# The second matrix of an MLP in seven half-block products, with weight sums formed in DRAM

## The chip, the core and the metric

The kernel runs on one core of a Trainium2 chip. Its time is the device time of one execution in microseconds; lower is better. A core has five engines which run side by side and wait for one another by semaphores: TensorE (PE in the profile) multiplies matrices, VectorE (DVE), ScalarE (ACT) and GpSimd (POOL) work element by element, SyncE (SP) issues transfers. Transfers (DMA) are issued on an engine's queue, in order with what that engine does, and are carried out by 16 DMA engines. Products land in PSUM, which has eight banks of 128 x 512 float32; all else lies in SBUF, and the inputs in DRAM.

## The reference

The input is a sequence of 1024 tokens with 1024 features, and there are two layers. Each layer is a mixer and an MLP, each followed by a layer norm of the scaled residual:

```
for layer in range(2):
    mix = hybrid_mixer(x, ...) if layer == 0 else recurrent_mixer(x, ...)
    x = layer_norm(ALPHA * x + mix, ln1_g[layer], ln1_b[layer])
    h = relu(x @ w1[layer])                    # 1024 -> 4096
    x = layer_norm(ALPHA * x + (h * h) @ w2[layer], ln2_g[layer], ln2_b[layer])   # 4096 -> 1024
```

The hybrid mixer joins windowed attention and a gated delta rule; the recurrent mixer is a gated branch beside a short convolution and a linear recurrence. All of it is float32. For each token half and layer the MLP is two products: 512 x 1024 by 1024 x 4096, and 512 x 4096 by 4096 x 1024.

## The kernel before, in words

**Two halves as two streams.** The 1024 tokens are cut into two halves of 512 (c = 0 and c = 1). `stream(c)` is a Python generator that emits, in order, a half's hybrid mixer, output projection and layer norm (`mix_out`), first MLP and norm (`mlp_ln`), four recurrent blocks (`rec_block`), their output projection and norm, and the second MLP and norm. The driver at the end of `trunk` takes turns between the two streams: a stream in phase 0 (a mixer) goes before one in phase 1 (first MLP) or 2 (second MLP), and of two in the same phase the first half goes first; in the recurrent blocks (`light`) the two change places after every unit. A generator that lacks a buffer or a condition yields `BLOCK`, and the other stream goes on; one that has finished a unit yields `UNIT`. So the MLP of one half lies between the products of the other half's mixer and fills the time in which those wait. Small pieces of work (layer norm, attention, the delta rule) are "mixers": generators that are asked first whenever a planner thinks their operands are there.

**The planner.** `Clock` keeps a rough model of the engines and gives every product a place in one fixed order on TensorE (`_pe`, a scheduling-only dependency on the product before). The other engines' orders come from the framework's scheduler; it is not bound to the order of emission.

**Products in float32 out of three.** TensorE runs a one-pass format (float32r). Every operand is split into a rounded part h and a rest l, and `mm3` (lines 359 to 362; the profile records the products at L204) issues h·h, h·l and l·h: three products of 128 x 128 by 128 x 512 for each block. `wblock` brings a weight stage of 128 x 1024 into one of three buffers `ws` on SyncE's queue, rounds it into `wh` (ScalarE, every fifth half on VectorE) and subtracts it into `wl` (VectorE and GpSimd in turn), in two halves of 512 columns; there are four half buffers of each. All instructions on the elementwise engines and all DMA issues are recorded at one line of the profile (L177), so they are told apart by tile names: `ws`, `wh`, `wl` weights; `g` the large buffers (activations, residuals); `s`, `t`, `f` rings of 128 x 512; `mm`, `mx` the two groups of four PSUM banks; `lns`, `lnw` norm statistics; `w` in a DMA stands for all MLP weights.

**The MLP** (`mlp`). It goes through eight parts e of 512 hidden units. For each, four projections by the first matrix, of eight `mm3` or 24 products each (`proj_fm`) give the hidden units; ScalarE takes relu and square, GpSimd squares again in float32, VectorE takes the rest l. Then for each of two column halves of the output, two weight stages with 16 `mm3`, 48 products, follow, summed in four banks; VectorE adds each bank to the residual `y`. In the last part of the very last MLP the order is turned, so that the final norm can start with the first 128 tokens.

**The norm** (`layernorm`). Statistics come with the last additions; then passes on VectorE, ScalarE and GpSimd; then 32 transposes on TensorE, after which ScalarE and VectorE split each bank into h and l for the next product.

**What the change touches**: `wblock`, `mm3`, `proj_fm`, `mlp`, `out_proj`, `rec_block`, `mix_out`, `mlp_ln`, `stream`, the planner's DMA entry, the rings' sizes, and the layout of w2 in DRAM.

Of the kernel before, what the change touches and what calls it, by code (L numbers as in the profile page):

```python
# [27 lines left out]
WB, HV, LG = 4, 5, 2  # L28
RINGS = dict(t=11, s=9, f=4)
# [29 lines left out]
class Clock:  # L59
    """Orders the tensor engine's work by a rough model of the engines: when each product's operands will be there."""  # L60
# [103 lines left out]
    def engine(self, eng, key):  # L164
        clk = self

        class Engine:
            def __getattr__(self, op):
                f = getattr(eng, op)

                def call(*a, **k):
# [6 lines left out]
                    if op == "dma_start":  # L178
                        clk.issue("D", outs, ins, max(0.06, aps[0].nbytes() / 360e3), 0.0, 2.0)
                        return r  # L180
# [20 lines left out]
    def matmul(self, out, lhsT, rhs, start, stop):  # L201
        n = int(np.prod(rhs.shape[1:]))
        c = 0.00042 * n * (1 if rhs.dtype == F32R else 4) if lhsT.shape[-1] > 32 else 0.046
        return self._pe(self.pe.matmul(out, lhsT, rhs, start=start, stop=stop), out, [lhsT, rhs], c, start)  # L204
# [6 lines left out]
def trunk(ctx: ExitStack, tc, I, out):  # L211
# [3 lines left out]
    DS, DA = clk.engine(nc.sync, "V"), clk.engine(nc.scalar, "V")  # L215
# [32 lines left out]
    def tl(r, dt=F32):  # L248
        return take(r, tpool.tile([P, 516], dt, tag=r, name=nm(r), bufs=RINGS[r]))

# [88 lines left out]
    def wblock(src, n=1024, hl=None):  # L339
        st = clk.tile("ws", 3, wpool.tile([P, 1024], F32, tag="ws", name=nm("ws"), bufs=3))[:, :n]  # L340
        DS.dma_start(st, src)
        m = n // 2
        if hl is None:
            hl = [clk.tile(t, WB, wpool.tile([P, 512], F32R, tag=t, name=nm(t), bufs=WB))[:, :m] for _ in range(2) for t in ("wh", "wl")]
        for i in range(2):
            h, l = hl[2 * i:2 * i + 2]
            a = st[:, i * m:(i + 1) * m]
            wcount[0] += 1
            if wcount[0] % HV == 0:
                V.tensor_copy(h, a)  # L350
            else:
                S.copy(h, a)
            if wcount[0] % LG == 0:
                G.tensor_tensor(l, a, h, ALU.subtract)
            else:
                V.tensor_tensor(l, a, h, ALU.subtract)
        return ([hl[0], hl[2]], [hl[1], hl[3]])

    def mm3(ps, lh, ll, rh, rl, start, stop):
        PE.matmul(ps, lh, rh, start=start, stop=False)  # L360
        PE.matmul(ps, lh, rl, start=False, stop=False)
        PE.matmul(ps, ll, rh, start=False, stop=stop)
# [34 lines left out]
    def load_xT(c, x, k2):  # L397
# [5 lines left out]
        else:  # L403
            st = clk.tile("ws", 3, wpool.tile([P, 1024], F32, tag="ws", name=nm("ws"), bufs=3))[:, :1024]
# [7 lines left out]
    def proj_fm(src, x, bank=None):  # L412
        wh, wl = wblock(src)
# [86 lines left out]
    def mlp(layer, yT, yg, ls, res=None):  # L500
        w1, w2 = I[f"w1_{layer}"], I[f"w2_{layer}"]
        for e in range(8):
            sh, sl = [], []
            yield from need("s", 9)
            wb, own = [], []
            if e == 7 and res is not None:
                yield from need("g", 4)
                for b in range(4):
                    t = gran(F32R)
                    own.append(t)  # L510
                    wb.append(wblock(w2[e * 4 + b], hl=[t[:, i * 512:(i + 1) * 512] for i in range(4)]))
            for f in range(4):
                ps = yield from proj_fm(w1[e * 4 + f], yT)
                h, l, r = ts("s", F32R), ts("s", F32R), ts("s")
# [4 lines left out]
                free("s", r)  # L519
                sh.append(h)  # L520
                sl.append(l)
                if e == 7 and f == 3:
                    yT.free()
                yield UNIT
            if e == 7 and res is not None:
                for n in range(NT):
                    a, b = n * P, (n + 1) * P
                    for half in range(2):
                        ps = mm_ps()
                        for f in range(4):  # L530
                            wh, wl = wb[half * 2 + f // 2]
                            mm3(ps, sh[f][:, a:b], sl[f][:, a:b], wh[f % 2], wl[f % 2], f == 0, f == 3)
                            yield
                        y = ytile(yg, n)[:, half * 512:(half + 1) * 512]
                        V.tensor_tensor(y, y, ps, ALU.add)
                        V.bn_stats(ls[:, n, 6 * half:6 * half + 6], y)
                    res["n"] = n + 1
                    if n == 0:
                        res["start"]()
                    yield UNIT  # L540
                free("g", *own)
                free("s", *sh, *sl)
                return
            for half in range(2):
                ps = [mm_ps() for _ in range(NT)]
# [790 lines left out]
```

## Time and profile before

| | |
|---|---|
| time, median of 3 runs | 2387.01 us (2386.92 to 2388.69) |
| span of the profiled execution, first to last instruction | 2384.5 us |
| mean granted TensorE clock | 0.992 |
| instructions | 33354 |
| moved by DMA | 227.43 MB, mean 95 GB/s |
| HBM read, written | 216.89 MB, 8.39 MB |

The profiled execution has no time of its own apart from its span; the 2.5 us between the span and the median lie around the first and the last instruction. The page gives each engine's busy time, its share of the span and its count of instructions. PEld is the loading of the stationary operand, which overlaps the products. In a row of a group the fields are: line, engine, operation, tile written <- tiles read, sizes, count | busy time in us, mean ns of one | idle time of the engine just before them <- what ended it. A row of the chain of waits has who waited, for whom, the total in us, how often, and the longest. In a row of a stretch, the count of instructions follows each engine's busy time. In a row of the timeline, start and length in us come first. In 40 equal slices of the span PE is at 90% or more in all but the first three, the seventh and the last.

```
PE   8889997999999999999999999999999999999997
DVE  7697659565754463755664623455665543633345
ACT  5364424443333242454443322344554232322331
POOL 3342334232332243433443432343333333433341
```

### The profile page before, as it was taken

The page shows a single profiled execution, that of the slowest core. Times are in us where ns is not written, and L with a number is a line of the kernel's source. Part 1 is how long each engine was busy: PE and PEld are TensorE (multiplying, and loading weights), DVE is VectorE, ACT ScalarE, POOL GpSimd, SP SyncE. Part 2 cuts the span into 40 slices and gives each one's busy share as a digit, 9 for nine tenths or more (in the row PEclk, how much of TensorE's full clock was granted, in tenths as well). Part 3 has the DMA queues.
Part 4 walks back from the last instruction along what each step waited for, and adds up shares of the span by engine and source line. Part 5 has one row for each costly group of instructions (what it writes and reads, how often), then busy time and mean ns, then how long its engine had stood idle before and what let it go on. Part 6 is the DMA issues. An engine that isn't in the chain of part 4 may idle for free. (4 is left out here: it accounts for less than half of the span.)

```text
span 2384.5 us, 33354 instructions
## 1 busy us (share of the span) xinstructions
PE 2298.9 (96%) x12724; PEld 1841.9 (77%) x12724; DVE 1345.1 (56%) x2550; ACT 912.7 (38%) x1813; POOL 843.0 (35%) x706
## 2 busy tenths in 40 slices
PE   8889997999999999999999999999999999999997
PEld 7666775677777878778887788877887788778876
DVE  7697659565754463755664623565665543633345
ACT  5364424443333242454443322344554232322331
POOL 3342334232332243433443432343333333433341
PEclk9999998999999999999999999999999999999999
DMA  4121231122233222322333222232325222332231
GB/s 154 54 81 31 81 124 36 54 69 74 73 114 110 95 88 98 123 89 97 98 131 125 82 96 97 97 121 91 98 93 177 85 97 97 107 115 98 98 117 51
DMA packets 67487, 227.43 MB, mean 95 GB/s; under 512 B 7424, under 2 KB 7808, under 8 KB 67328
## 3 DMA queue, kind: packets, MB, share of 16 engines
q1 hardware_dynamic: 58832, 204.01, 25.9%
q10 hardware_dynamic: 8496, 21.30, 2.5%
q8 instruction: 100, 1.64, 0.3%
q14 instruction: 59, 0.48, 0.1%
HBM read 216.89 MB, written 8.39 MB: 94 GB/s over the span
## 5 line engine op out<-in xcount | busy, mean ns | idle before, releaser
L177 POOL TENSOR_TENSOR wl<-ws,wh 128x512 fp32r<-128x512 f32 (+1 forms) x372 | 497.6, 1338 | 1261.4 <-ACT wh L177 979.4
L204 PE MATMUL mm<-g,wh 128*128 128x512 f32 x2816 | 886.7, 396 | 0.5 <-DVE g L177 0.5
L177 ACT CAST wh<-ws 128x512 fp32r<-128x512 f32 (+1 forms) x595 | 365.5, 616 | 993.0 <-PE mm L204 910.1
L204 PE MATMUL mm<-wh,s 128*128 128x512 f32 x1984 | 648.2, 399 | 11.4 <-ACT s L177 5.7
L204 PEld LDWEIGHTS mm<-g,wh 128*128 128x128 f32 x2816 | 520.2, 189 | 107.2 <-issue 2.9
L204 PE MATMUL mm<-g,wl 128*128 128x512 f32 x1408 | 550.9, 391 | 5.4 <-POOL wl L177 5.4
L204 PEld LDWEIGHTS mm<-wh,s 128*128 128x128 f32 x1984 | 374.0, 189 | 102.6 <-ACT s L177 6.2
L204 PE MATMUL mm<-wl,s 128*128 128x512 f32 x992 | 391.9, 395 | 2.3 <-POOL wl L177 1.4
L177 DVE TENSOR_TENSOR wl<-ws,wh 128x512 fp32r<-128x512 f32 (+1 forms) x372 | 281.2, 756 | 188.8 <-ACT wh L177 184.4
L204 PEld LDWEIGHTS mm<-g,wl 128*128 128x128 f32 x1408 | 265.1, 188 | 64.0 <-POOL wl L177 7.1
L204 PE MATMUL mm<-wh,g 128*128 128x512 f32 (+1 forms) x768 | 235.2, 380 | 10.0 <-ACT wh L177 6.1
L177 DVE TENSOR_TENSOR s<-s,s 128x512 fp32r<-128x512 f32 x128 | 100.4, 784 | 242.9 <-POOL s L177 231.1
L204 PEld LDWEIGHTS mm<-wl,s 128*128 128x128 f32 x992 | 187.4, 189 | 43.3 <-POOL wl L177 1.8
L177 DVE TENSOR_TENSOR g<-g,mm 128x512 f32<-128x512 f32 x224 | 144.0, 680 | 130.7 <-PE mm L204 130.5
L204 PEld LDWEIGHTS mm<-wh,g 128*128 128x128 f32 x768 | 142.0, 190 | 38.7 <-ACT wh L177 6.1
L177 DVE CAST wh<-ws 128x512 fp32r<-128x512 f32 (+1 forms) x149 | 73.8, 495 | 172.6 <-PE mm L204 165.0
L177 POOL TENSOR_TENSOR s<-s 128x512 f32<-128x512 f32 x128 | 145.3, 1135 | 26.4 <-ACT s L177 26.4
L204 PE MATMUL mm<-wl,g 128*128 128x512 f32 (+1 forms) x384 | 143.7, 374 | 0.1
L177 ACT ACTIVATE s<-mm 128x512 f32<-128x512 f32 x128 | 75.9, 593 | 62.1 <-PE mm L204 61.9
L177 ACT ACTIVATE s<-s 128x512 fp32r<-128x512 f32 (+1 forms) x136 | 83.5, 614 | 19.0 <-DVE s L177 8.0
L204 PEld LDWEIGHTS mm<-wl,g 128*128 128x128 f32 x384 | 72.9, 190 | 11.9 <-DVE wl L177 0.4
L204 PE MATMUL mx<-g,wh 128*128 128x512 f32 x256 | 78.8, 389 | 0.0
(209 smaller groups left out, 2230.3 us busy)
## 6 DMA issues: line engine op xcount, KB each, us to landing
ws<-w SPq DMA_DIRECT2D x256, 512.0 KB, 3.3
ws<-hin_fm SPq DMA_DIRECT2D x32, 512.0 KB, 3.3
ws<-rin SPq DMA_DIRECT2D x32, 512.0 KB, 3.3
ws<-hout SPq DMA_DIRECT2D x16, 512.0 KB, 3.4
ws<-rout SPq DMA_DIRECT2D x16, 512.0 KB, 3.4
t<-ln ACTq DMA_DIRECT2D x28, 256.0 KB, 4.2
ws<-hin_q SPq DMA_DIRECT2D x8, 512.0 KB, 3.2
g<-x ACTq DMA_DIRECT2D x8, 512.0 KB, 5.0
```

Of the source, the lines that this page charges most:

```text
L177: r = f(*a, **k)
L204: return self._pe(self.pe.matmul(out, lhsT, rhs, start=start, stop=stop), out, [lhsT, rhs], c, start)
```

## The change

**The second matrix in seven products.** A block j is two parts e: 1024 hidden units. Its product, 512 tokens by 1024 units by 1024 columns, is cut in two along each of the three: A (units by tokens) into a11, a12, a21, a22 and the weights into b11, b12, b21, b22. Instead of eight quarter products there are seven (`seven`), each of 256 tokens by 512 units by 512 columns, 24 products of TensorE: two weight stages, two chunks of 128 units each, two token tiles, three products. The activation sides are combined on VectorE in place (four combinations of 128 x 1024); the weight sides are four sums and differences t1 to t4 which are formed beforehand. Partial results stay in PSUM (two banks X of the `mm` group, two banks R of `mx`), later products add to them, and VectorE adds or subtracts a bank to the residual after each product.

**Hidden units kept raw.** For such a block `hidden` keeps the squared hidden units in float32 in two large buffers, and the split into h and l is made for each product of the seven (ScalarE copy and VectorE subtract of 128 x 512, twice per product). GpSimd has no part in it: the weight subtracts of `hidden` and `seven` are all on VectorE.

**Woven.** `weave` emits one unit of the next block's first matrix (24 products) and then two units of the present block's seven (12 products each). The last block of an MLP has no next one; in the last MLP of the second half `ends` and `finish` take the place of the turned order of before, and part 6 goes first in the old way.

**Which blocks.** An MLP goes part by part in the old way (`straight`) until e is even, two large buffers are free, and, for the first half, the second half's output projection of the same layer has been emitted; the rest goes in blocks of seven products.

**Sums in DRAM.** `w2_sums` is started as a mixer with the first MLP. For each layer and block it copies a quarter of w2 (1 MiB) into each of t1 to t4 on SyncE's queue, then adds further quarters by accumulating DMAs on GpSimd's queue (four, then two, then one), with the planner's clock between them.

**Order of the stages.** The recurrent blocks of the second half no longer wait until the first half's are done, but for the same block of the first half; they use ring `s`. The second half's norm before an MLP (`hold`), and the first half's norm after its first MLP, wait until the other half has emitted the last product of its first matrix.

**Weight stages.** `wblock` casts and subtracts 1024 columns at once, with three buffers of 1024 instead of four of 512. Ring `s` has 10 tiles instead of 9; a pair of tiles `r` is new; the descriptor scratch for GpSimd's DMAs is set to 2048 bytes.

```diff
-WB, HV, LG = 4, 5, 2
-RINGS = dict(t=11, s=9, f=4)
+WB, WS, HV, LG = 3, 3, 5, 2
+RINGS = dict(t=11, s=10, f=4)
...
+    def split(h, l, x, key):
+        wcount[0] += 1
+        (V.tensor_copy if wcount[0] % HV == 0 else S.copy)(h, x)
+        (G if key else V).tensor_tensor(l, x, h, ALU.subtract)
...
+        split(h, l, st, pool and wcount[0] % LG)
...
+    SUMS = dict(t1=("b11", "b12"), t3=("b12", "b22"), t2=("b11", "b12", "b22"), t4=("b11", "b12", "b22", "b21"))
...
+        for layer, j in ((i, j) for i in range(2) for j in range(4)):
+            for k, (first, *_) in SUMS.items():
+                behind(DS.dma_start(rows(tsum[layer][j][k]), rows(w2_quarter(layer, j, first))))
+                t = clk.now + 4.0
+                yield lambda: t
+            for i in range(1, 4):
+                t = clk.now + 10.0
+                yield lambda: t
+                for k, v in SUMS.items():
+                    if i < len(v):
+                        behind(DG.dma_start(rows(tsum[layer][j][k]), rows(w2_quarter(layer, j, v[i])), accum_op=ALU.add,
+                                            max_dma_last_dim=2048))
+            summed.add((layer, j))
+            t = clk.now + 8.0
+            yield lambda: t
...
+        def hidden(f, z):
+            ps = yield from proj_fm(w1[f], yT, mm_ps, False)
+            used()
+            S.activation(z, ps, AF.Relu)
+            S.activation(z, z, AF.Square)
+            yield UNIT
...
+            for i, (a, b, acc, out, sign, last) in enumerate((
+                    ("a12", "b21", "R", (0, 0), 1, False), ("a11", "b11", "X", (0, 0), 1, True),
+                    ("a21", "t1", "R", (1, 1), 1, False), ("a21", "t2", "X", (0, 1), -1, False),
+                    ("a12", "b22", "R", (0, 1), 1, True), ("a21", "t3", "X", (1, 1), -1, True),
+                    ("a22", "t4", "X", (1, 0), 1, True))):
+                if i == 2:
+                    V.tensor_tensor(A["a21"], A["a21"], A["a22"], ALU.subtract)
...
+                for p in range(2):
+                    yield from wait(lambda: either(2))
...
+                    S.copy(ah2, x)
+                    V.tensor_tensor(al2, x, ah2, ALU.subtract)
+                    wh, wl = wblock(w2_quarter(layer, j, b)[p * P:(p + 1) * P], pool=False)
+                    for k in range(2):
+                        for t in range(2):
+                            mm3(bank[acc][t], ah2[:, k, t * P:(t + 1) * P], al2[:, k, t * P:(t + 1) * P], wh[k], wl[k],
+                                start and p + k == 0, p + k == 2, not start)
+                            if p + k == 2:
+                                accumulate(bank[acc][t], 2 * out[0] + t, out[1], sign, done and last)
...
+        if res is not None:
+            yield from straight(6, False)
+        while e < 8 and not ((c == 1 or sts[1].get("op", -1) >= layer) and rings["g"] >= 2 and e % 2 == 0):
+            yield from straight(e, e == 7)
+            e += 1
+        if e < 8:
+            n = 3 if res is not None else 4
+            yield from first(e // 2)
+            for j in range(e // 2, n):
+                nxt = first(j + 1) if j + 1 < n else ends() if res is not None else None
+                yield from weave(nxt, seven(j, hids.pop(j), j == 3), 2)
...
+        s["ln0"]["op"] = which // 2
...
+        yield from wait(hold)
...
+                if c == 0:
+                    yield from wait(lambda: "m7" in sts[1])
...
-            yield from rec_block(c, b, s["x"], hT, s)
+            yield from wait(lambda: c == 0 or sts[0].get("rb", 0) > b)
+            yield from rec_block(c, b, s["x"], hT, s, "ts"[c])
+            st[c]["rb"] = b + 1
...
-    nc = _bacc.Bacc("TRN2", target_bir_lowering=False, num_devices=1)
+    nc = _bacc.Bacc("TRN2", target_bir_lowering=False, num_devices=1, dynamic_dma_scratch_size=2048)
```

More of the change, by code (lines that the diff above doesn't have):

```diff
@@ new lines, in mlp, with accumulate, used, straight @@
+    def mlp(layer, c, yT, yg, ls, res=None):
+        w1 = I[f"w1_{layer}"]
+        seen = set()
+        def accumulate(ps, n, half, sign, done):
+            y = ytile(yg, n)[:, half * 512:(half + 1) * 512]
+            op = ALU.add if sign > 0 else ALU.subtract
+            if (n, half) not in seen:
+                seen.add((n, half))
+                V.scalar_tensor_tensor(y, y, ALPHA, ps, ALU.mult, op)
+            else:
+                V.tensor_tensor(y, y, ps, op)
+            if done:
+                V.bn_stats(ls[:, n, 6 * half:6 * half + 6], y)
+        either = lambda n: next((r for r in "st" if rings[r] >= n), None)
+        left = [32]
+        def used():
+            left[0] -= 1
+            if left[0] == 0:
+                yT.free()
+                st[c]["m7"] = layer
+        def straight(e, done):
+            j, i = divmod(e, 2)
+            yield from wait(lambda: either(8))
+            ring = either(8)
+            own = [(ts(ring, F32R), ts(ring, F32R)) for _ in range(4)]
@@ L544, in mlp @@
             for half in range(2):
+                yield from wait(lambda: kept[0] == 0)
                 ps = [mm_ps() for _ in range(NT)]
                 for p in range(2):
-                    wh, wl = wblock(w2[(e * 2 + half) * 2 + p])
-                    for j in range(2):
-                        f = 2 * p + j
+                    wh, wl = wblock(w2_quarter(layer, j, f"b{i + 1}{half + 1}")[p * P:(p + 1) * P])
+                    for k in range(2):
+                        h, l = own[2 * p + k]
@@ L567, in out_proj @@
+        if res is not None:
+            yield from finish()
     def out_proj(w, oT, resid, yg, ls):
```

252 lines of the change are left out of this document (150 added, 102 removed).

## The prediction

> **What bounds the kernel now.** I read the page's totals first, then the busy time by stretch, then what TensorE waited for.
>
> ```profile
> span 2384.5 us, 33354 instructions
> PE 2298.9 (96%) x12724; PEld 1841.9 (77%) x12724; DVE 1345.1 (56%) x2550; ACT 912.7 (38%) x1813; POOL 843.0 (35%) x706
> ```
>
> TensorE (PE) is busy for 2298.9 of 2384.5 us, so 85.6 us are idle in all, and no edit that only hides waits can win more than that. The runs' median, 2387.0, is 2.5 us above the span; I add those 2.5 us at the end.
>
> ```profile
> 986.00:1250.00 264.00, 260.35 (x1143) 212.96 (x1144) 153.29 (x195) 125.95 (x205) 104.10 (x94) 1.00 0.32 108
> 2100.00:2300.00 200.00, 200.00 (x874) 163.81 (x873) 64.02 (x105) 57.95 (x96) 65.70 (x55) 1.00 0.29 95
> 350.00:800.00 450.00, 430.03 (x3173) 331.75 (x3173) 278.70 (x639) 171.37 (x426) 145.84 (x122) 0.98 0.23 77
> ```
>
> Columns: stretch, length, busy time and count of PE, PEld, DVE, ACT, POOL, then granted clock, DMA share, GB/s. 2100 to 2300 is MLP alone: PE never rests, at full granted clock, and 874 products in 200 us give a pitch of 0.229 us per 512-column product. DVE is at 32% there. Only fewer products shorten such a stretch.
>
> ```profile
> PE mx L207 <- DVE g L177: 9.4, 5, 6.7
> PE mm L204 <- ACT s L177: 8.6, 4, 2.9
> PE mm L204 <- POOL wl L177: 6.8, 5, 1.8
> ```
>
> No wait of PE totals 10 us. What stands in line behind PE is therefore spare: that is the cover which the change draws on.
>
> **The change, part by part.**
>
> *Products removed.* A block j (1024 hidden units, two e's) now costs 2 x 96 = 192 products in the second matrix; seven half-blocks of 24 cost 168. So each j done in this way saves 24 x 0.229 = 5.5 us of PE. How many are there? The second token half has them all in layer 0 (4) and three in layer 1. The first half goes the old way, e by e, until the second half's output projection has been ordered, and switches at the next even e. The SyncE queue shows where that falls in layer 0:
>
> ```profile
> 350.97 120.62 SPq L177 DMA_DIRECT2D ws<-w  x11
> 518.59 44.13 SPq L177 DMA_DIRECT2D ws<-w  x7
> 577.04 0.33 SPq L177 DMA_DIRECT2D ws<-w  x1
> 608.22 39.42 SPq L177 DMA_DIRECT2D ws<-w  x7
> 661.85 31.74 SPq L177 DMA_DIRECT2D ws<-w  x5
> 701.32 53.59 SPq L177 DMA_DIRECT2D ws<-w  x9
> 761.25 40.03 SPq L177 DMA_DIRECT2D ws<-hout  x8
> 806.39 165.26 SPq L177 DMA_DIRECT2D ws<-w  x30
> ```
>
> 11+7+1+7+5+9 = 40 MLP blocks, 8 to an e, go before the second half's output matrix: five e's. Then e = 5 is odd and goes straight, and only e = 6, 7 (j = 3) is left: 1. In layer 1 the second half's recurrent blocks now run one block behind the first half's, so I take j = 0 straight and 3 in the new form. Sum 1+4+3+3 = 11 (bounds 10 and 12): 264 products, 60.4 us. PE falls to 2238.5.
>
> *Work added on DVE, ACT and POOL.* Rows of 2100 to 2300, where DVE and POOL hardly overlap:
>
> ```profile
> L177 DVE TENSOR_TENSOR wl<-ws,wh 128x512 fp32r<-128x512 f32 x36 | 24.8, 688 | 16.0 <-ACT wh L177 15.6
> L177 DVE TENSOR_TENSOR g<-g,mm 128x512 f32<-128x512 f32 x36 | 23.0, 681 | 35.4 <-PE mm L204 35.4
> L177 DVE CAST wh<-ws 128x512 fp32r<-128x512 f32 x15 | 6.9, 462 | 30.9 <-PE mm L204 30.9
> L177 ACT CAST wh<-ws 128x512 fp32r<-128x512 f32 x58 | 36.1, 622 | 133.7 <-PE mm L204 133.7
> L177 ACT ACTIVATE s<-s 128x512 fp32r<-128x512 f32 x19 | 12.0, 633 | 0.6
> L177 POOL TENSOR_TENSOR wl<-ws,wh 128x512 fp32r<-128x512 f32 x37 | 47.9, 1294 | 137.5 <-ACT wh L177 107.2 <-DVE wh L177 18.3 <-issue 8.3
> ```
>
> And of other stretches (the first kv_proj, then the whole run):
>
> ```profile
> L177 DVE TENSOR_TENSOR wl<-ws,wh 128x264 fp32r<-128x264 f32 x4 | 1.7, 429 | 0.0
> L177 DVE TENSOR_TENSOR wl<-ws,wh 128x512 fp32r<-128x512 f32 x364 | 277.3, 762 | 187.3 <-ACT wh L177 182.9
> L177 DVE TENSOR_TENSOR g<-g,t 128x512 f32<-128x512 f32 x53 | 59.7, 1170 | 0.8 <-ACT g L177 0.7
> L177 DVE TENSOR_TENSOR g<-mx,g 128x512 fp32r<-128x512 f32 x56 | 36.7, 678 | 9.9 <-ACT g L177 9.6
> L177 DVE TENSOR_TENSOR lnw<-lnw 128x4 f32<-128x4 f32 x36 | 11.5, 319 | 1.0
> L177 DVE BATCH_NORM_STATS2 lns<-g 128x6 f32<-128x512 f32 x64 | 42.1, 679 | 0.1
> L207 PE MATMUL mx<-csb,g 128*128 128x128 f32 x312 | 47.3, 281 | 13.3 <-DVE g L177 9.4 <-DVE t L177 3.9
> ```
>
> From 429 ns at 264 columns to 688 at 512 is 1.04 ns a column, so the new 1024-wide subtract is about 1.22 us. One of the 14 units of a block in the new form (12 products, 2.75 us of PE) asks of DVE: weight subtract 1.22 (POOL does none of them here); subtract of the activation half 0.69; one accumulate 0.68; a fifth of a 1024-wide cast, at most 2 x 0.46 / 5 = 0.18; its share of four 1024-wide combinations, 4 x 1.22 / 14 = 0.35. Sum 3.12 us, more than PE's 2.75. Woven with the next block's first matrix (two units to one of 24 products: 11.0 us of PE) DVE asks 2 x 3.12 + 1.22 + 0.18 = 7.6 us, 69%: hidden. ACT: three casts of about 1.2 for four fifths of the time, two copies of 0.62, and two activations of 0.63, some 5.5 of 11.0: hidden too.
>
> The last block of an MLP has nothing to be woven with; there the cover is gone. That comes three times (both halves in layer 0, first half in layer 1), and each time the other half's layer norm, now held until the last first-matrix product is out, falls beside it. DVE: 14 x 3.12 = 43.7, statistics 8 x 0.68 = 5.4, the norm's eight splits 8 x 0.68 = 5.4: 54; of this about 3 may trail and about 6 is done ahead (three weight buffers). PE: 168 x 0.229 + 32 transposes x 0.15 = 43.3. Stall 54 - 9 - 43 = 2, plus some 2 where products six and seven share banks without a gap. If the norm's own passes (eleven of 512 columns at 1.17, and some 13 of four columns at 0.32: 17) also fall there, it is 21. Does DVE do those early? Loads of the norm's parameters say that queues are filled well ahead:
>
> ```profile
> L177 ACTq DMA_DIRECT2D t<-ln x28: 334/335/685, 720.7 to 1903.7; - x28
> ```
>
> The first came at 720.7, 40 us before that half's output matrix was even loaded (761.25). So I take 7 each, 21 in all, and keep 12 and 63.
>
> The last MLP ends with six units alone (6 x 0.37 = 2) and four splits after them: 4 us (0 to 8).
>
> A DVE subtract takes 688 ns where POOL rests and 762 over the run. The Trainium skill's SBUF — State Buffer, "Who interferes with whom", says that a VectorE instruction with two SBUF inputs and a GpSimd one reading SBUF exclude each other for a whole instruction; the two rows agree with it. By it DVE runs at 688 where POOL has no subtracts; at 762 a solo stage would be some 3 us longer, 9 in the sum.
>
> *Recurrent blocks side by side.* Before, each half's recurrent blocks ran beside MLP. In 986 to 1250 PE was busy 260.4 us; four blocks of 120 products are 110, MLP the other 150. MLP takes 0.32 us of DVE and 0.29 of ACT per us: 48 and 44. That leaves at most 105 of DVE and 82 of ACT for four blocks: 26 and 21 for 27.5 us of PE. Two streams of these fill DVE to 95% where MLP left slack. The two output projections and the norm lie among them, and the 26 holds pieces of a norm. Price 10 us (0 to 35).
>
> *Sums in DRAM.* Per layer and block four 1 MiB copies on SyncE's queue and seven 1 MiB accumulating DMAs on POOL's, in eight rounds paced at 4x4 + 3x10 + 8 = 54 us by the planner's clock, from about 350 on: in the second half's mixer.
>
> ```profile
> q1 hardware_dynamic: 58832, 204.01, 25.9%
> ws<-w SPq DMA_DIRECT2D x256, 512.0 KB, 3.3
> ```
>
> 204 MB took 25.9% of 16 engines for 2384.5 us: 3.0 us per MB, 3.2 per MiB. If an accumulate costs like a copy, a round is 11 x 3.2 = 35 us beside 12 of present traffic (share 0.23): it fits into 54. Nothing here shows an accumulate; if it costs twice (it reads two, writes one), a round is 57 + 12 = 69. On SyncE weight loads queue behind a copy for 3 to 6 us; three stages are loaded ahead of units of 5.5 us: hidden. On POOL an accumulate waits for the landing of the one before it on its tile; behind it stand half of the other weight subtracts, the squares of the straight MLP and the mixer's convolution adds. PE waits once the stay exceeds some 16 us of prefetch. Bounds: 0 and 8 x 15 = 120, if the round of four (4 x 6.3 = 25 against 10) always reaches PE. I take 10, near the copy's row.
>
> *Other edits.* Splits 1024 wide take fewer instructions but come later (POOL 2.5 us); three buffers of 1024 instead of two cover that. The new form loads 14 stages of 512 KiB per block instead of 8: woven 3 per 11 us (143 GB/s), solo one per 3.1 us (169), against the 330 GB/s that 3.0 us per MB make, each landing 3.3 us after its issue: hidden, except beside the sums, where C has it. The new rings cost nothing that a row shows.
>
> **Sum.** PE 2238.5 + idle (85.6 + 21 + 4 + 10 + 10 = 130.6) = 2369, and 2.5: 2371.5 us, 15.5 less (0.65%).
>
> **Rivals.** A: DVE's idle time swallows it all; solo stages, recurrent stage and sums cost at most 15. Then 2387 - 60.4 - 5.5 (a twelfth block) + 15 = 2336; range 2322 to 2345. For it: no wait of PE above 10 us now. Against: the 3.12 over 2.75.
>
> B: the norm's passes stay behind the solo blocks on DVE, 21 each and 63 in all, and the recurrent stage costs 15 for the same reason: 2387 - 60.4 + 63 + 4 + 15 + 5 (sums) = 2414, slower. It decides as soon as solo stage and norm together ask DVE for over some 55 us in PE's 43. For it: 95% in the recurrent stage. Against: 720.7.
>
> C: accumulates cost twice. Each round runs 15 us over its pace, POOL stays, half of it reaches PE: 8 x 7.5 = 60 in place of 10: 2371.5 + 50 = 2421 (2405 to 2480). The Trainium skill's DMA: Bandwidth & Descriptors, "Specifications", gives about 358 GB/s of HBM per core; by its figure, with both reads and the write counted, a round of some 30 MB would be an estimated 85 us, which speaks for C. No run yet shows it.
>
> D: the change does less than it says, since the first half's condition fails in both layers: 7 blocks, 38 us, against one solo stage (7), 4, 10 and 10: 2380; with the last two somewhat dearer 2380 to 2392, hardly a change. For it: five e's of eight were already gone at 761.
>
> **How the numbers follow.** Less than 0.2% (4.8 us) is what a measurement of this kernel can hardly tell from nothing. Forecast (2345 to 2382) 0.42, A 0.20, B 0.16, C 0.12, D 0.10. Faster 0.42 + 0.20 = 0.62, same 0.10, slower 0.28. The range 2325 to 2425 leaves out a little of A and half of C, the upper part; the likeliest case alone is 2345 to 2382.
>
> **What would show it.** PE's count near 12724 - 264 = 12460 and busy near 2238; pitch still 0.229 in woven stretches, DVE near 70% there. Idle of PE ahead of `wl` or of the activation halves in three stretches of 45 us; PE waits on `t`, `f` and `s` in the recurrent stage. POOL waiting on DMA between 350 and 800, with PE's wait on POOL `wl` small: if that wait is tens of us, C. If the three solo stretches lose over 15 us each, B. If PE's count is above 12520, D. I am wrong outright if the woven stretches lose pitch.

## The result, and the profile after

The changed kernel takes 2555.0 us (median of 4 runs, 2551.7 to 2557.7) against 2387.9 us beside it: a ratio of 1.0698, with an interval from 1.0683 to 1.0713. It is 7% slower, 130 us above the top of the predicted range.

The totals of the page after, then the same stretch of both kernels, 400 to 1100 us, in which most of the sums are formed (they end at 1129; lines L178, L206 and L210 of this kernel are L177, L204 and L207 of the one before; columns as before: length, busy time and count of PE, PEld, DVE, ACT, POOL, then granted clock, DMA share, GB/s).

```profile
span 2550.3 us, 32067 instructions
PE 2259.9 (89%) x12460; PEld 1812.6 (71%) x12460; DVE 1550.8 (61%) x2537; ACT 1004.6 (39%) x1723; POOL 561.3 (22%) x399
```

```profile
400.00:1100.00 700.00, 685.47 (x4214) 542.31 (x4213) 400.27 (x790) 258.66 (x547) 238.78 (x200) 1.00 0.27 88
```

```profile
400.00:1100.00 700.00, 527.78 (x3399) 408.76 (x3400) 272.91 (x564) 172.18 (x359) 192.20 (x143) 0.87 0.75 184
1200.00:1400.00 200.00, 200.00 (x884) 165.59 (x883) 127.51 (x146) 88.37 (x119) 0.00 (x0) 1.00 0.42 140
```

The count of products, 12460, is the predicted one to the last product. PE's idle time went from 85.6 us to 2550.3 - 2259.9 = 290.4, and between 400 and 1100 from 14.5 to 172.2: 157.7 of the 204.8 us lie there. No compute engine is near full in that stretch; the DMA engines are at a share of 0.75, to which the experiments come back. In the woven stretch (last row) nothing is wrong: PE never rests, 884 products in 200 us are a pitch of 0.226, and DVE is at 64% where 69% was forecast.

What is POOL doing between 400 and 1100? Some of its longest waits over the whole run, then the first accumulating DMAs in the timeline (start, length, instruction, and in brackets the idle time before it and what ended it):

```profile
POOL wl L178 <- ACT wh L178: 666.0, 59, 266.2
POOL t L178 <- issue: 303.1, 38, 19.3
...
POOL t L178 <- DMA t<-w: 56.3, 9, 13.6
```

```profile
443.50 1.17 POOL L178 DMA_DIRECT2D t<-w  x1
453.79 1.05 POOL L178 DMA_DIRECT2D t<-w  x1 [9.13 <-issue]
464.32 1.02 POOL L178 DMA_DIRECT2D t<-w  x1 [9.48 <-issue]
472.89 1.03 POOL L178 DMA_DIRECT2D t<-w  x1 [7.55 <-issue]
473.55 1.44 POOL L178 TENSOR_TENSOR g<-g,asc 128x512 f32<-128x512 f32 x1
```

The first four accumulates go to four different tiles and have nothing of each other to wait for. They were meant to take 4 x 1 us of POOL's queue; they take 30 us, from 443.5 to 473.5. POOL is shown busy for 1 us of each, and for the other 7.5 to 9.5 it is idle with "issue" as the end of it: the engine waited for nothing that the profile shows. Over the run that is 303.1 us, while the wait that the prediction had priced, for the landing of the accumulate before on the same tile, is only 56.3. The Trainium skill's Perfetto Trace Analysis, "DMA Instruction — SWDGE (GPSIMD)", says that such a row ends when the descriptors have been generated, not when the data have moved. The trace agrees that the row is no measure of the transfer (1.03 us against a median landing of 8.7 below), but it shows also that the row is no measure of how long the queue is held.

Who stands behind? The longest waits of the other engines between 400 and 1100:

```profile
DVE s L178 <- POOL r L178: 148.4, 15, 31.2
...
PE mx L206 <- DVE t L178: 62.8, 7, 24.3
PE mm L206 <- POOL wl L178: 51.3, 5, 19.8
PE mx L206 <- DVE S L178: 25.2, 1, 25.2
```

The longest are about as long as a round of four accumulates. More than half of it comes round a corner. `r` is the pair of tiles in which GpSimd squares the hidden units of the straight MLP; DVE waits 148.4 us for it, and what comes behind in DVE's order, the mixer's work, waits too: PE waits for `t` and for `S`, the state of the delta rule. The first such wait of PE, with one row from each of the three engines' timelines:

```profile
481.94 1.43 POOL L178 TENSOR_TENSOR r<-r 128x512 f32<-128x512 f32 x1
483.41 0.69 DVE L178 TENSOR_TENSOR s<-r,s 128x512 fp32r<-128x512 f32 x1 [27.53 <-POOL r L178]
484.41 1.22 PE L206 MATMUL mx<-S,t 128*128 128x128 f32 x4 [25.18 <-DVE S L178]
```

POOL reaches that square only behind the fifth accumulate; DVE has then stood for 27.53 us and PE for 25.18. The prediction's test for rival C, "PE's wait on POOL `wl`", reads tens of us and so points to C, but it sees only 51 us of a loss of 158.

The rest of the loss is slower products. The same 12460 products took 2233.1 us in the first experiment, whose stretch has no such idle, and 2259.9 here: 26.8 us more, with a granted clock of 0.87 between 400 and 1100. The Trainium skill's TensorE: Matmul & The Clock Gate, "Part 1: The HAM clock gate (the "warmup" mystery)", has the clock fall to half once the array has been idle for some 3.4 us; the row agrees in direction.

### The profile page after: what moved, and what is told of

The parts are those of the page before. It is cut to its first block, busy times and chain, and to the rows that moved or that the text cites. A ratio compares the mean times of both kernels' runs of the same rounds, so it can differ in the third digit from the quotient of the medians.

```text
span 2550.3 us, 32067 instructions
## 1 busy us (share of the span) xinstructions
PE 2259.9 (89%) x12460; PEld 1812.6 (71%) x12460; DVE 1550.8 (61%) x2537; ACT 1004.6 (39%) x1723; POOL 561.3 (22%) x399
## 3 DMA queue, kind: packets, MB, share of 16 engines
q0 software_dynamic: 29568, 58.72, 13.6%
## 4 chain that ended last, share of the span: by engine, by line
PE 58%; DVE 18%; issue 13%; ACT 4%; POOL 3%; DMA 1%; ACTq 0%; DVEq 0%; POOLq 0%
PE mm L206 46%; PE mx L206 11%; DVE g L178 6%; DVE t L178 3%; DVE s L178 2%; DVE wl L178 2%; POOL t L178 1%; DVE f L178 1%; DVE lnw L178 1%; ACT wh L178 1%; DVE hsc L178 1%; PE mx L210 1%; POOL wl L178 1%; ACT t L178 1%; ACT s L178 1%
## 5 line engine op out<-in xcount | busy, mean ns | idle before, releaser
L206 PE MATMUL mm<-g,wh 128*128 128x512 f32 x2816 | 892.4, 398 | 3.4 <-DVE g L178 3.4
L178 ACT CAST wh<-ws 128x1024 fp32r<-128x1024 f32 (+1 forms) x350 | 364.8, 1042 | 766.8 <-PE mm L206 676.5
L178 DVE TENSOR_TENSOR wl<-ws,wh 128x1024 fp32r<-128x1024 f32 (+1 forms) x335 | 418.9, 1252 | 336.2 <-ACT wh L178 331.6
L206 PEld LDWEIGHTS mm<-g,wh 128*128 128x128 f32 x2816 | 524.3, 190 | 113.5 <-DVE g L178 5.0
L206 PE MATMUL mm<-g,wl 128*128 128x512 f32 x1408 | 553.7, 393 | 31.8 <-POOL wl L178 30.6
L178 POOL TENSOR_TENSOR wl<-ws,wh 128x1024 fp32r<-128x1024 f32 (+1 forms) x103 | 259.0, 2514 | 978.0 <-ACT wh L178 666.0
L206 PE MATMUL mm<-wh,s 128*128 128x512 f32 x1216 | 405.9, 401 | 13.3 <-DVE g L178 5.0
L206 PEld LDWEIGHTS mm<-g,wl 128*128 128x128 f32 x1408 | 267.0, 190 | 90.5 <-POOL wl L178 31.4
L206 PEld LDWEIGHTS mm<-wh,s 128*128 128x128 f32 x1216 | 233.1, 192 | 65.6 <-issue 4.4
L206 PE MATMUL mm<-wl,s 128*128 128x512 f32 x608 | 241.2, 397 | 5.3 <-POOL wl L178 3.8
L206 PE MATMUL mm<-wh,g 128*128 128x512 f32 (+1 forms) x768 | 234.8, 384 | 9.1 <-ACT wh L178 6.3
L206 PE MATMUL mx<-wh,s 128*128 128x512 f32 x528 | 171.9, 392 | 1.7 <-DVE s L178 1.7
L206 PEld LDWEIGHTS mm<-wh,g 128*128 128x128 f32 x768 | 144.1, 193 | 36.5 <-ACT wh L178 6.3
L206 PE MATMUL mm<-wl,g 128*128 128x512 f32 (+1 forms) x384 | 145.8, 380 | 17.1 <-POOL wl L178 16.9
L178 POOL DMA_DIRECT2D t<-w x56 | 57.9, 1034 | 362.0 <-issue 303.1
L206 PEld LDWEIGHTS mm<-wl,s 128*128 128x128 f32 x608 | 116.7, 192 | 29.0 <-POOL wl L178 4.2
L178 DVE TENSOR_TENSOR s<-g,s 128x512 fp32r<-128x512 f32 x158 | 110.3, 714 | 43.4 <-ACT s L178 43.3
L178 ACT CAST s<-g 128x512 fp32r<-128x512 f32 x158 | 95.7, 623 | 100.5 <-PE mm L206 46.5
L178 DVE TENSOR_TENSOR s<-r,s 128x512 fp32r<-128x512 f32 x32 | 28.3, 885 | 158.2 <-POOL r L178 158.2
L206 PEld LDWEIGHTS mx<-wh,s 128*128 128x128 f32 x528 | 99.3, 188 | 23.3 <-DVE s L178 3.0
L178 DVE CAST wh<-ws 128x1024 fp32r<-128x1024 f32 x88 | 63.3, 720 | 78.2 <-PE mm L206 66.4
L178 DVE TENSOR_TENSOR g<-g,mm 128x512 f32<-128x512 f32 x140 | 91.9, 682 | 28.7 <-PE mm L206 28.4
```

Of the source, the lines that this page charges most:

```text
L178: r = f(*a, **k)
L206: ins = self.pe.matmul(out, lhsT, rhs, start=start, stop=stop, skip_group_check=fresh)
```

## The experiments

Two theories of the 8-us stay. **R, room**: GpSimd writes a transfer's descriptors into the scratch that the change sets to 2048 bytes, and holds its queue until earlier ones have been carried out and there is room. **P, time per descriptor**: writing the descriptors of one 1 MiB transfer in 2048-byte pieces takes GpSimd some 8 us. Rival to both is **traffic**: what the sums move (rival C) holds up everything else. And there is the question whether the rest of the change does what was forecast.

**No sums.** `w2_sums` issues nothing; the products with t1 to t4 read a plain quarter of w2 in their place.

```diff
-        return tsum[layer][j][q] if q in SUMS else I[f"w2_{layer}"][j * 4 + QUARTER[q]]
+        q = SUMS.get(q, (q,))[0]
+        return I[f"w2_{layer}"][j * 4 + QUARTER[q]]
...
```

> The changed kernel without any weight sums: no copies, no accumulating DMAs; where a product wants a sum it reads the first quarter of it, so the output is not the reference's. All else stays. Theory Q (the sums as a whole cost about 158 us of idle TensorE and some 20 of lower clock between 400 and 1100 us): 2370 to 2390 us, about the time before. Theory S (the new order of the stages is what costs, the sums merely lie there): above 2480.

2363.1 us, ratio 0.9898 (0.9883 to 0.9912), 7 below the range expected of it.

```profile
span 2361.1 us, 31952 instructions
PE 2233.1 (95%) x12460; PEld 1796.4 (76%) x12460; DVE 1552.9 (66%) x2537; ACT 1004.2 (43%) x1723; POOL 508.6 (22%) x343
```

So the sums cost 2555.0 - 2363.1 = 192 us: in the spans, 162.4 of PE's idle time and the 26.8 by which its products are slower. Without its 10 us for the sums the prediction gave 2361.5, so what it got wrong in the total is in that one term; the other terms are wrong too, but cancel (below).

**The same traffic on SyncE's queue.** Each accumulating DMA becomes a plain copy of the same quarter to the same place, so t1 to t4 are not the sums.

```diff
-                        behind(DG.dma_start(rows(tsum[layer][j][k]), rows(w2_quarter(layer, j, v[i])), accum_op=ALU.add,
-                                            max_dma_last_dim=2048))
+                        behind(DS.dma_start(rows(tsum[layer][j][k]), rows(w2_quarter(layer, j, v[i]))))
```

> The changed kernel with each accumulating DMA replaced by a plain 1 MiB copy to the same place on SyncE's queue: the same transfers in number and nearly in bytes, nothing on GpSimd's queue (the sums are wrong, so the output is not the reference's). Theories P and R (GpSimd's queue is what hurts): 2380 to 2410 us. Theory D (traffic): 2480 or more.

2364.8 us, ratio 0.991 (0.9889 to 0.9931): 1.7 us above no sums at all, within both intervals, and 15 below the range expected. 88 transfers of 1 MiB, all on the queue of the weight loads, cost nothing that can be told from zero. A copy doesn't read what it writes over, so this is not the whole traffic: the accumulates of the changed kernel took 13.6% of 16 engines for 2550.3 us, 347 us for 56 transfers or 6.2 each, about twice the 3.2 of the prediction's plain copy. Rival C's premise, an accumulate at twice a copy, is right for the 2048-byte pieces; what the doubled traffic costs is seen below, where nothing stays at issue.

**Longer pieces.** A limit of 8192 bytes on a transfer's last dimension in place of 2048: a quarter as many descriptors. R and P both expect the stay to go or shrink.

```diff
-                                            max_dma_last_dim=2048))
+                                            max_dma_last_dim=8192))
```

> The changed kernel with accumulating DMAs cut into pieces of 8192 bytes instead of 2048: a quarter of the descriptors, the same bytes. Theory P (GpSimd's stay of 8.6 us per accumulating DMA is time per descriptor, spent by GpSimd itself): stay near 3 us, 2420 to 2450 us. Theory R (GpSimd waits for room in the 2048-byte descriptor scratch, 33 entries a DMA now and 9 then): no stay beyond the 1.0 us shown, about 2385. Theory D (the transfers fill the 16 DMA engines and weight loads come late): bytes are the same, 2540 or more.

2417.4 us, ratio 1.0125 (1.011 to 1.014): just under P's range, and 32 above the 2385 of R. In the timeline the four go out back to back, and POOL's next stay is for a landing:

```profile
447.95 3.48 POOL L178 DMA_DIRECT2D t<-w  x4
457.39 1.47 POOL L178 TENSOR_TENSOR g<-g,asc 128x512 f32<-128x512 f32 x1 [5.96 <-ACT g L178]
467.97 0.82 POOL L178 DMA_DIRECT2D t<-w  x1 [9.11 <-DMA t<-w]
```

```profile
POOL t L178 <- DMA t<-w: 190.2, 27, 13.1
```

The accumulates of the second and third group come 10 us of the planner's clock after the first, but the landing now takes 12.1 us (median), and POOL stands. The 192 us thus fall into two parts: 138 that go with the stay at issue (2555.0 to 2417.4) and 54 that are left (2417.4 to 2363.1). Two things stand in the 54, and the runs don't divide them. One is the wait for landings with POOL's work behind it: between 400 and 1100 DVE waits 38.2 us for `r`, against 14.0 without sums. The other is traffic: ACT waits 42.2 us there for weights that land late, against none without sums, and the chain of waits that ended last gives 3% of the span to each of the two landings, accumulates and weights.

**R or P: the sums in the kernel before, with two sizes of scratch.** The kernel before gets `w2_sums` as the change has it, 2048-byte pieces and all, with nobody reading the sums; once with 16384 bytes of scratch and once with 2048. The pieces are the same, so P expects the same stay in both.

```diff
...
+        if c == 0:
+            spawn(w2_sums())
...
-    nc = _bacc.Bacc("TRN2", target_bir_lowering=False, num_devices=1)
+    nc = _bacc.Bacc("TRN2", target_bir_lowering=False, num_devices=1, dynamic_dma_scratch_size=16384)
```

> The kernel before with the same sums beside it (same copies, accumulating DMAs of 2048-byte pieces, same pacing), which nothing reads, and with 16384 bytes of descriptor scratch instead of 2048. Theory P: GpSimd stays about 8.6 us at each accumulating DMA all the same, and the time is 2480 to 2560. Theory R: room for some thirty DMAs, so the stay falls to about 1 us and the time to 2390 to 2410. Theory D: about as P in time, but with GpSimd's stay gone and SyncE's loads landing late. Theory S: 2390.

> The kernel before with the sums beside it, unread, pieces of 2048 bytes, as in the run with 16384 bytes of scratch, but now with 2048 bytes of descriptor scratch: the scratch is all that differs from that run (2461 us, stay of 1.0 us per accumulating DMA). Theory R (room in the scratch): GpSimd stays some 8 us at each accumulating DMA again and the time is 2510 to 2560. Theory P (time per descriptor): no change, 2461.

With 16384 bytes 2461.1 us, ratio 1.0311 (1.0295 to 1.0326); with 2048 bytes 2604.1, ratio 1.0906 (1.0884 to 1.0927). The first accumulates in the two timelines, 16384 first:

```profile
442.28 4.28 POOL L177 DMA_DIRECT2D t<-w  x4
451.30 1.47 POOL L177 TENSOR_TENSOR g<-g,asc 128x512 f32<-128x512 f32 x1 [4.74 <-DVE asc L177]
```

```profile
443.26 1.18 POOL L177 DMA_DIRECT2D t<-w  x1
452.14 1.04 POOL L177 DMA_DIRECT2D t<-w  x1 [7.70 <-issue]
460.64 1.01 POOL L177 DMA_DIRECT2D t<-w  x1 [7.47 <-issue]
469.21 1.03 POOL L177 DMA_DIRECT2D t<-w  x1 [7.55 <-issue]
```

The first time lies between the ranges of R and P and the second 44 above that of R, so the times alone decide nothing; the stay does. With room, 528 packets for each transfer (29568 packets of 56 transfers) are issued in 1.07 us. P falls: writing the descriptors is not what takes 8 us. R stands: only the scratch differs, and it costs 143 us in this kernel, much as the 138 in the changed one, with the same traffic on both sides. With the small scratch one accumulate follows the other by some 8.5 us, about the time in which one lands (9.3, median). The sums also harm the kernel before by 73 us without any stay. POOL waits 175.6 us for landings there, and PE's wait on POOL `wl` goes from 6.8 to 37.1 us; how much of the 73 comes in this way wasn't tested.

**How much room.** 4096-byte pieces with the 2048 bytes of scratch, in the changed kernel; one run.

```diff
-                                            max_dma_last_dim=2048))
+                                            max_dma_last_dim=4096))
```

> The changed kernel with pieces of 4096 bytes (half the descriptors). Theory R says that GpSimd stays as soon as the descriptors of the DMAs in flight do not fit: with 8192-byte pieces four went out without a stay, with 2048 the second already stayed. In between: the first two or three of a group of four go out 1 us apart and the last stays; time 2420 to 2480. Theory P (time per descriptor): each of the four stays about half as long as with 2048, 4 us.

2423.8 us. Three accumulates go at once, and the fourth does not:

```profile
447.46 2.85 POOL L178 DMA_DIRECT2D t<-w  x3
456.85 0.90 POOL L178 DMA_DIRECT2D t<-w  x1 [6.54 <-DVE asc L178]
521.41 2.74 POOL L178 DMA_DIRECT2D t<-w  x3
530.50 0.88 POOL L178 DMA_DIRECT2D t<-w  x1 [6.35 <-issue]
```

In the first group the profile puts the fourth's idle time down to DVE, but in each of the seven groups behind it to "issue": 47.9 us in 7 waits. The packets of the page's queue rows (8064, 15232 and 29568 for 56 transfers on 16 engines) are 9, 17 and 33 for each transfer and engine, with 8192, 4096 and 2048 bytes. Four times 9 fit, three times 17 fit, four times 17 and two times 33 don't: by an estimate from these counts, 2048 bytes of scratch hold between 51 and 65 packets for each engine. If the room grows with the bytes, 16384 hold 12 to 15 transfers of 33 packets, not the "some thirty" expected above.

**Spreading the landings.** First by more time: 8192-byte pieces and 25 us of the planner's clock before each group.

```diff
-                t = clk.now + 10.0
+                t = clk.now + 25.0
...
```

> The changed kernel with pieces of 8192 bytes and 25 us instead of 10 before each group of accumulating DMAs. Theory L (what is left of the cost with 8192-byte pieces, 54 us, is GpSimd waiting in order for the group before to land, 12 us and more, with its other work behind it): the waits on landings nearly vanish and the time comes to 2363 to 2378, faster than the kernel before. Rival: accumulating DMAs cost otherwise, by their traffic on DRAM: 2400 to 2417 as with 10 us.

2402.2 us, ratio 1.0059 (1.0044 to 1.0074): above the range of the theory that landings are all that is left, and inside that of its rival, traffic. The waits on landings didn't vanish either; they grew from 190.2 us:

```profile
POOL t L178 <- DMA t<-w: 309.6, 26, 71.5
```

But 263.9 of them lie after 900 us, where POOL has little else to do, and between 400 and 1100 DVE waits for `r` no longer than without sums (12.2 us). The loss is no longer where it was. Two stretches, the first as above, the second where seven-product blocks have begun; the latter of this kernel and of the one without sums:

```profile
400.00:1100.00 700.00, 677.92 (x4155) 533.16 (x4156) 402.76 (x724) 251.69 (x470) 185.11 (x137) 0.99 0.68 196
900.00:1250.00 350.00, 329.49 (x1416) 264.91 (x1416) 215.72 (x263) 142.70 (x198) 24.82 (x25) 0.98 0.75 224
```

```profile
900.00:1250.00 350.00, 347.11 (x1542) 285.99 (x1541) 233.59 (x283) 156.08 (x214) 8.51 (x5) 1.00 0.42 142
```

At this pace the sums last to 1339 us. From 900 on the new form loads 14 stages a block, and beside the sums those come late: ACT waits 62.1 us for the landing of weights in this stretch. PE idles 17.6 us more there than without sums, of 20.8 in the whole run (148.8 against 128.0). So traffic does cost, where it meets a stage with much of its own.

```profile
ACT wh L178 <- DMA ws<-w: 42.8, 11, 5.5
ACT wh L178 <- DMA ws<-t: 19.3, 5, 7.1
```

Then one by one: 8192-byte pieces, an accumulate every 9 us of the planner's clock, never two in a row on one tile, the next block's copies between them.

```diff
+            for n, (k, i) in enumerate((("t4", 1), ("t2", 1), ("t1", 1), ("t4", 2), ("t2", 2), ("t3", 1), ("t4", 3))):
+                t = clk.now + 9.0
+                yield lambda: t
+                behind(DG.dma_start(rows(tsum[layer][j][k]), rows(w2_quarter(layer, j, SUMS[k][i])), accum_op=ALU.add,
+                                    max_dma_last_dim=8192))
+                if n in (1, 2, 4, 5):
+                    copy()
```

> The changed kernel with pieces of 8192 bytes and the accumulating DMAs one by one, 9 us apart by the planner's clock, alternating over t4, t2, t1, t4, t2, t3, t4 so that the same sum comes again only after two or more others; the copies of the next block between them. Theory L (order on GpSimd's queue: waits for landings): GpSimd waits little, the sums end near 950 us, 2366 to 2385, faster than the kernel before. If traffic costs as soon as it lies beside the blocks of seven products: 2385 to 2405.

2384.5 us (10 runs), ratio 0.9984 (0.9975 to 0.9994): with the whole computation done, the fastest of the versions, at the top of the range expected, and below the kernel before by less than the 0.2% that the prediction called hardly to be told from nothing. The sums end at 1022 us, POOL waits 87.2 us for landings (7 times), and the sums cost 21 us in place of 192. Which part of this edit does it (one by one, the order of the tiles, the place of the copies) wasn't tested.

**The rest of the change.** Three kernels on the structure, all without sums. In the first every block goes the old way (`straight`), in the new order of stages, with the new splits and buffers; in the second the order of the stages is put back too; the third has the seven products and lets GpSimd take every second weight subtract again (it reads plain quarters, as the first experiment does).

```diff
+        for e in range(8 if res is None else 7):
+            yield from straight(e, e == 7)
...
```

> The changed kernel without sums and without the seven products: every block goes the old way (8 x 24 products), the order of the stages, the holds, the recurrent blocks side by side and the wider splits stay. TensorE's count is 12724 again. Against 2363 with eleven blocks in seven products: if these are worth their 60 us less three solo stages of 7 and 4 at the end, 2395 to 2405; if the new order costs nothing beside the kernel before, 2385 to 2390; if the solo stages cost 21 each, 2355 to 2365.

```diff
...
-            yield from wait(lambda: c == 0 or sts[0].get("rb", 0) > b)
...
-            yield from rec_block(c, b, s["x"], hT, s, "ts"[c])
+            yield from rec_block(c, b, s["x"], hT, s, "t")
...
```

> The run with all blocks in the old way and no sums (2420 us, 32 above the kernel before), with the order of the stages put back as far as possible: the first half's norm after its first MLP and the second half's norms no longer wait, and the second half's recurrent blocks wait until the first half's are done, all in ring t, so that each half's recurrent blocks lie beside the other's MLP. Theory O (the side-by-side recurrent blocks and held norms cost the 32): 2385 to 2398. Rival (the wider splits and new buffers cost it): 2410 to 2422.

```diff
-            ps = yield from proj_fm(w1[f], yT, mm_ps, False)
+            ps = yield from proj_fm(w1[f], yT, mm_ps)
...
```

> The changed kernel without sums, and with the weight subtracts of the woven and solo stages shared between VectorE and GpSimd, as elsewhere, instead of all on VectorE. If VectorE's load makes the remaining waits (solo stages, the norm after the second half's first MLP, 24 us in one place): 2340 to 2355. If the two get in each other's way, or the waits are others: 2363 or more.

All straight, new order: 2420.4 us, ratio 1.0135 (1.012 to 1.015), above all three ranges expected. Old order put back: 2401.9, ratio 1.0057 (1.0041 to 1.0074). The seven products are therefore worth 2420.4 - 2363.1 = 57 us, the new order costs about 18.5, and what is left of the change in the second kernel (the wider splits, the buffers and rings) the other 13.5, so that this kernel lies just above the range expected of it. Where the order costs, the stretch from 1300 to 1600 shows, for the kernel before, for all straight in the new order, for the old order put back, and for the one without sums:

```profile
1300.00:1600.00 300.00, 294.44 (x1306) 240.14 (x1305) 146.08 (x236) 98.55 (x164) 110.52 (x87) 0.99 0.30 99
```

```profile
1300.00:1600.00 300.00, 269.70 (x1176) 218.64 (x1175) 213.94 (x259) 185.29 (x265) 105.37 (x77) 0.95 0.31 106
```

```profile
1300.00:1600.00 300.00, 291.57 (x1307) 240.16 (x1306) 145.36 (x203) 92.84 (x124) 104.61 (x59) 0.99 0.31 102
```

```profile
1300.00:1600.00 300.00, 257.32 (x1123) 208.27 (x1122) 232.48 (x280) 179.30 (x256) 108.97 (x73) 0.94 0.32 107
```

PE idles 5.6, 30.3, 8.4 and 42.7 us: in the new order both halves' recurrent blocks and a norm stand there with no MLP left to fill. With GpSimd's share given back 2373.0, ratio 0.9933 (0.9916 to 0.995): DVE's busy time falls from 1552.9 to 1467.3 us, and yet the kernel is 10 us slower. A subtract of 1024 columns takes 2522 ns on POOL and 1251 on DVE, and the activation subtract `s<-g,s` on DVE goes from 716 to 877 ns; which of the two costs the 10 us wasn't tested. To take load off VectorE in this way wins nothing.

## Why the prediction was wrong

The step that failed is the term "Sums in DRAM": 10 us with bounds of 0 and 120, where the runs show 192. It was not only a wrong size. The prediction let an accumulate hold POOL's queue for the landing of the one before it on its tile, and for nothing else. This wait is real; beside late weights it stands in the 54 us that are left with 8192-byte pieces. The larger part, 138 us, it had no place for: GpSimd holds its queue at the issue itself when the scratch has no room for the descriptors, so that a transfer of 33 packets an engine waits for the one before it, whatever the tile (38 of the 56 have idle time put down to "issue" before them). The edit that causes it, scratch of 2048 bytes, the prediction doesn't name: it stands at nothing, without a reason. No row of the trace before could show it, since that kernel issued nothing from GpSimd's queue in this way. The upper bound of 120 counted one stay for each round of four; one landing of 6.3 us for each accumulate, 56 x 6.3 = 353 us of POOL, would have been the warning.

The test for where it reaches PE was right in its first half: a round of four holds POOL for 30 us, longer than the "some 16 us of prefetch", and reaches PE. The second half was not: it comes mostly by way of DVE, which stands for the straight MLP's squares with the mixer's work behind them, and the 26.8 us of slower products were not in the sum.

Point by point:

- Products removed: 11 blocks, x12460, as forecast, and 2233.1 us of PE without sums (2238.5).
- Work on DVE: the 1024-wide subtract 1.25 us (1.22), woven stretches 64% (69%), no loss of pitch. POOL's 2.5 us is 2.52.
- Solo stages and the end, 21 + 4: too dear. Without sums PE idles 2361.1 - 2233.1 = 128.0 us, all straight in the same order 2421.2 - 2296.7 = 124.5. The seven products add 3.5 us of idle in all, not 25.
- Recurrent blocks side by side, 10 (0 to 35), and the splits, 0: too cheap. All straight against before is 124.5 - 85.6 = 38.9 us of idle. In time the order's 18.5 us lie within its bounds; the splits and buffers, put at nothing, cost 13.5, and what in them stays open. The errors, 21.5 us too much and 28.9 too little, nearly cancel, so that the structure's forecast, 2361.5, meets the 2363.1 measured partly by luck.
- Rivals. B was half right on place (the row below is of the kernel without sums: 24.1 us at 1371 to 1396 us in one wait for DVE's norm), not on size; and with all blocks straight a like wait for the norm is still 16.3 us, so that most of it needs no solo block. D falls with the count, A with the 2363.1. Rival C had the right engine, the right stretch and the right sign, at 60 us, and its premise on the traffic holds; but the same transfers as plain copies cost 1.7 us, and the whole traffic, spaced, 21. By the figure of the Trainium skill's DMA: Bandwidth & Descriptors, "Specifications", a round was an estimated 85 us, which spoke for it. The trace with 8192-byte pieces doesn't bear it out: there the first seven rounds start 65 to 78 us apart, beside the rest of the traffic. The runs show that the stay at issue came first, and that late weight loads cost PE most where the sums ran into the seven products.

```profile
PE mx L210 <- DVE g L178: 32.3, 10, 24.1
```

## What to carry to other kernels

An accumulating DMA on GpSimd's queue has three prices here: its row, the time for which it holds the queue at issue, and the wait for a landing. The profile shows the first as busy time and the second only as idle time "ended by issue"; look for it there, and count the packets of a transfer against the size of the scratch before that is made smaller. Ask also what stands behind such a stay on the engines that wait for this one, for that is where most of the loss was. When such transfers must share a queue with work that others need, space them one by one so that the one waited for has landed, and end them before the next stage that needs the bandwidth: 2384.5 us here against 2417.4 and 2402.2.

## What the runs showed of the hardware

- A DRAM-to-DRAM accumulate of 1 MiB lands after 8.7 us (median; 9.3 in the kernel before) where the stay at issue keeps the next one back, and after 11.8 to 12.9 us in the runs where the next can start sooner. Its packets took 13.6% of 16 engines for 58.72 MB, 5.9 us per MB, about twice the 3.0 of the plain transfers before; in 8192-byte pieces it was 12.1% of a span of 2417.2 us, or 5.0. Rows of the changed kernel, the first with the median from issue to landing last:

```profile
t<-w POOLq DMA_DIRECT2D x56, 1024.0 KB, 8.7
q0 software_dynamic: 29568, 58.72, 13.6%
```

- The longest step of the chain of waits that ended last, after TensorE and VectorE, has no engine at all: "issue" is 13% of 2550 us, against 3% without the sums. Most of that is the stay:

```profile
PE 58%; DVE 18%; issue 13%; ACT 4%; POOL 3%; DMA 1%; ACTq 0%; DVEq 0%; POOLq 0%
```

- Idle time of TensorE had a second price here: the 162 us that the sums added came with 27 us of slower products, at a granted clock of 0.949 over the run against 0.984.
